# Making a feed-forward pair's weight sums ahead of another operand's chain, and putting off one K tile of wO

## The chip, the cores and the metric

The kernel runs on one core of a Trainium2 chip. The metric is the device time of one execution in microseconds (us), the median of the runs shown. A core has TensorE (PE in the profile, with its weight loads as PEld), VectorE (DVE), ScalarE (ACT), GpSimd (POOL) and SyncE (SP), which issues most DMAs. Each engine takes its instructions in one fixed order and waits on semaphores for the others.

## The reference

One transformer block on 512 tokens of width 1024, in fp32:

```python
h = rmsnorm(x, norm_mix_pre)
... = split_cols(h @ w_in)                       # attention, gated MLP, conv and pool branches, gates
merged = gates[0]*y_a + gates[1]*y_b + gates[2]*y_c + gates[3]*y_d
x = x + rmsnorm(merged @ w_out, norm_mix_post)
h = rmsnorm(x, norm_ffn_pre)
f = jnp.square(jax.nn.relu(h @ w_ff1)) @ w_ff2   # 1024 -> 4096 -> 1024
x = x + rmsnorm(f, norm_ffn_post)
```

The change lies in `merged @ w_out` (in the kernel: wO) and in the first part of the feed-forward layer.

## The kernel before, in words

Every fp32 operand is split in two parts, a rounded high part (`wh`, `hh`, `uh`, ..., made by an ACT cast) and the rest (`wl`, `hl`, `ul`, ..., made by a DVE subtraction). A product is three matmuls, high by high, high by low and low by high (`mm3`). `split_w` makes such a pair of a weight tile of 128x1024 that `load` has brought into one of three `raw` buffers; `wh` and `wl` have five buffers each. Every one of these casts has the line L95 in the profile, that of a helper, so rows are told apart by the names of their tiles.

wO: for each half of the output columns (`hf`) four weight tiles are loaded and split, and for each of four token tiles t, 24 matmuls (8 K tiles by three) run into a PSUM bank `wo`. The left operand of K tile k is the merged activation `mT[k]` (`mh`, `ml`); the one of k = 7 is the last that the gates' loop makes, by a chain of DVE operations on `g` (L538, L540), an ACT cast to `mh` and a DVE subtraction to `ml` (L544).

Then the feed-forward layer. The first four blocks of 128 features (`EARLY = 4`) are made in the plain way: `ff1` runs on the first 256 tokens while the norm of the last token tile is under way, and on the other 256 tokens after it (PSUM tiles `z`). The other 28 blocks are made in pairs by `seven`, a scheme of seven products in place of eight for two feature blocks by two halves of K by two halves of the tokens. It needs sums of the activations (`hsum`, made by `halve`, and `S4`) and sums of the weights. The weights of a pair are loaded as `left` and `rght`; each is split as it is (`w`, `w22`), then four DVE subtractions in place (L344 to L347) turn both into sums, and these are split again (`wl`, `wr`; as tiles also called `wh` and `wl`). PE then runs the parts `pa` (A11 by w), `pb` (A12 by w), `pc` (S1 by the sums of left), `pa` (S2 by the sums of rght), `pd` (A22), `pc` (S4 by `w22`), `pa` (S3). S4 is made before the loop, in two halves in the buffers of `u[-2:]` (called `u30` and `u31` in the order below), by three DVE steps each (L962 to L964), and cast and split into a free part of `h2` (`hh`, `hl`, L973). Between the parts of a pair, `second()` runs the second feed-forward matmul of an earlier block (PSUM tiles `acc`); in the first pair after the parts n = 1, 2 and 4.

Only PE's order (and ACT's in one early stage) is that of the program. On DVE and ACT a scheduler sets it before the run, by the order in the program and its own estimate of when each operand is ready. So what stands earlier in the program tends to be earlier on the engine, and an operation in an engine's order holds back all that stand behind it.

Of the kernel before, what the change touches and what calls it, by code (L numbers as in the profile page):

```python
# [13 lines left out]
AF = mybir.ActivationFunctionType  # L14
# [4 lines left out]
P = 128  # L19
S = 512  # L20
NT = S // P
D = 1024
KD = D // P
# [57 lines left out]
def build(ctx, tc, d, out):  # L81
# [20 lines left out]
    PE, ACT = InOrder(nc.tensor, True), InOrder(nc.scalar, False)  # L102

    def f(t):
        return t.bitcast(F32)
# [4 lines left out]
    def load(src, n=1024):  # L110
        raw = wp.tile([P, 1024], F32, tag="raw", name="raw", bufs=3)
        nc.sync.dma_start(raw[:, :n], src)
        return raw

    def split_w(raw, n=1024):
        hi = wp.tile([P, 1024], F32R, tag="wh", name="wh", bufs=5)
        lo = wp.tile([P, 1024], F32R, tag="wl", name="wl", bufs=5)
        ACT.copy(hi[:, :n], raw[:, :n])
        DVE.tensor_tensor(lo[:, :n], raw[:, :n], f(hi)[:, :n], ALU.subtract)  # L119
        return hi, lo  # L120
# [14 lines left out]
    def weights(src, n=1024):  # L135
        return split_w(load(src, n), n)

    def mm3(ps, lhs, rhs, start, stop, more=False):

        k = dict(skip_group_check=more)  # L140
        PE.matmul(ps, lhs[0], rhs[0], start=start, stop=False, **k)
        PE.matmul(ps, lhs[0], rhs[1], start=False, stop=False, **k)
        PE.matmul(ps, lhs[1], rhs[0], start=False, stop=stop, **k)

    def sl(pair, *ix):
        return pair[0][ix], pair[1][ix]
# [26 lines left out]
    def k0(n):  # L173
        return c0[:, C0[n][0]:C0[n][1]]
# [11 lines left out]
    def bank(name):  # L186
        return mm.tile([P, 512], F32, tag="mm", name=name)

    ps = bank("warm")
# [94 lines left out]
    for (a, b), xt, wa in zip(groups, xts, was):  # L284
        if a == 1:
            angles = rope_tables()
        for k in range(a, b):
            g = k0("gpre")[:, k:k + 1]
# [39 lines left out]
    HK, HS = KD // 2, S // 2  # L328
    B1, B2 = slice(0, 512), slice(512, 1024)

    def part(ps, w, at, a, first):

        for k in range(HK):
            mm3(ps[:, :HS], sl(w, slice(None), slice(at + k * P, at + (k + 1) * P)), sl(a, slice(None), k),
                first and k == 0, k == HK - 1, not first)

    def seven(srcs, forms, small, g, h, by_dma):

        A11, A12, A22, S1, S2, S3, S4 = forms
        left, rght = load(srcs[0]), load(srcs[1])  # L340
        w = split_w(left)
        w22 = split_by_dma(srcs[1][:, B2], rght[:, B2], 512) if by_dma else split_w(rght[:, B2], 512)

        DVE.tensor_tensor(left[:, B1], rght[:, B1], left[:, B1], ALU.subtract)  # L344
        DVE.tensor_tensor(rght[:, B1], rght[:, B2], rght[:, B1], ALU.subtract)
        DVE.tensor_tensor(rght[:, B2], rght[:, B2], left[:, B1], ALU.subtract)
        DVE.tensor_tensor(left[:, B2], left[:, B2], rght[:, B2], ALU.subtract)  # L347
        wl = split_w(left)
        wr = split_w(rght)
        pa, pb = bank("pa"), bank("pb")  # L350
        part(pa, w, 0, A11, True)
        x1 = small()
        ACT.copy(x1, pa[:, :HS])
        yield
        part(pb, w, 512, A12, True)
        DVE.tensor_tensor(g[:, :HS], pb[:, :HS], x1, ALU.add)
        yield
        pc = bank("pc")
        part(pc, wl, 0, S1, True)
        x5 = small()  # L360
        ACT.copy(x5, pc[:, :HS])
        yield
        part(pa, wr, 512, S2, False)
        x2 = small()
        ACT.copy(x2, pa[:, :HS])
        yield
        pd = bank("pd")
        part(pd, wl, 512, A22, True)
        yield
        part(pc, w22, 0, S4, False)  # L370
        DVE.tensor_tensor(h[:, :HS], pc[:, :HS], x2, ALU.add)
        yield
        part(pa, wr, 0, S3, False)
        x3 = small()
        ACT.copy(x3, pa[:, :HS])
        DVE.tensor_tensor(g[:, HS:], pd[:, :HS], x3, ALU.add)  # L376
        DVE.tensor_tensor(h[:, HS:], x3, x5, ALU.add)
        yield
# [245 lines left out]
    ps = bank("kr")  # L624
# [7 lines left out]
    for t in range(NT):  # L632
        ps = bank("q")
# [6 lines left out]
    for j in range(2):  # L640
        ps = bank("kn")
# [3 lines left out]
    for t in range(NT):  # L645
        ps = bank("v")
# [3 lines left out]
    for j in range(3):  # L650
        ps = bank("qT")
# [88 lines left out]
    mT = [], []  # L740
# [19 lines left out]
    def rest(steps):  # L760
        for _ in steps:
            pass
# [39 lines left out]
    ops = forms(z, zsum)  # L802
    w = split_by_dma(d["wB"][1], own=wbp)
    for b in range(2, KD):
        steps = merge(b - 1, w)
        for i in (0, 2):
            g, h = (gp.tile([P, S], F32, tag="g", name="g", bufs=6) for _ in range(2))
            for n, _ in enumerate(seven((d["wG"][4 * b + i], d["wG"][4 * b + i + 1]), ops, small_g, g, h, True)):
                if i == 0 and n in (1, 2, 4, 5):
                    next(steps)  # L810
                if i == 0 and n == 5:
                    rest(steps)
                    w = split_by_dma(d["wB"][b], own=wbp)
            for x in (g, h):
                DVE.tensor_tensor(x, x, rbc, ALU.mult)  # L815
            gates.extend((g, h))
# [36 lines left out]
    def ff1(j, w, ps, lo, hi):  # L853

        for c, parts in ((0, (0, 1)), (1, (0,))):
            for k in range(KD):
                for p in parts:
                    PE.matmul(ps[:, lo:hi], w[c][:, k * P:(k + 1) * P], h2[p][:, k, lo:hi],
                              start=c == 0 and k == 0 and p == 0, stop=c == 1 and k == KD - 1)

    def turn_h(t):
# [14 lines left out]
        DVE.tensor_scalar(stt[:, t, 3:4], stt[:, t, 3:4], 1.0 / D, EPS, ALU.mult, ALU.add)  # L876
        DVE.reciprocal(r2[:, t:t + 1], stt[:, t, 3:4])

    for hf in range(2):
        wo = [weights(d["wO"][hf, c]) for c in range(4)]  # L880
        for t in range(NT):
            ps = bank("wo")
            for k in range(KD):
                mm3(ps, sl([m[k] for m in mT], slice(None), slice(t * P, (t + 1) * P)),
                    sl(wo[k // 2], slice(None), slice((k % 2) * 512, (k % 2 + 1) * 512)), k == 0, k == KD - 1)
            cols = slice(hf * 512, (hf + 1) * 512)
            sq = wk_.tile([P, D], F32, tag="sq", name="sq", bufs=1)
            ACT.activation(sq[:, :512], ps, AF.Square, accum_out=stt[:, t, hf:hf + 1])
            DVE.tensor_tensor(yg[:, t, cols], ps, gmix[:, cols], ALU.mult)
            if hf == 0:  # L890
                DVE.tensor_scalar(stt[:, t, 0:1], stt[:, t, 0:1], D * EPS, None, ALU.add)
                continue
            if t:
                turn_h(t - 1)
            norm_scale(stt[:, t, 2:3], stt[:, t, 3:4], stt[:, t, 0:1], stt[:, t, 1:2])
            for c in (slice(0, 512), slice(512, D)):
                DVE.scalar_tensor_tensor(x1[:, t, c], yg[:, t, c], stt[:, t, 2:3], x1[:, t, c], ALU.mult, ALU.add)
                DVE.tensor_tensor(yg[:, t, c], x1[:, t, c], gffn[:, c], ALU.mult)
    EARLY = 4
    early = []  # L900
    for j in range(EARLY):
        if j == EARLY - 1:
            turn_h(NT - 1)
        w, ps = (split_by_dma if j < 2 else weights)(d["w1"][j]), bank("z")
# [20 lines left out]
    u = [up.tile([P, S], F32, name=f"u{j}") for j in reversed(range(NFF))][::-1]  # L925
# [4 lines left out]
    pend = []  # L930

    def usplit(j):
        uh = us.tile([P, S], F32R, tag="uh", name="uh")
        ul = us.tile([P, S], F32R, tag="ul", name="ul")
        ACT.copy(uh, u[j])
        DVE.tensor_tensor(ul, u[j], f(uh), ALU.subtract)  # L936
        return uh, ul
# [15 lines left out]
    def finish(j):  # L953
        ACT.activation(u[j], u[j], AF.Relu)
        ACT.activation(u[j], u[j], AF.Square)
        pend.append((j, usplit(j)))


    s4 = [x.rearrange("p (k t) -> p k t", k=2) for x in u[-2:]]
    for k, x in zip((0, 2), s4):  # L960
        a, b = slice(HK + k, HK + k + 2), slice(k, k + 2)
        DVE.tensor_tensor(x, f(hh_)[:, a, :HS], f(hsum[0])[:, 1, b], ALU.subtract)  # L962
        DVE.tensor_tensor(x, x, f(hl_)[:, a, :HS], ALU.add)
        DVE.tensor_tensor(x, x, f(hsum[1])[:, 1, b], ALU.subtract)  # L964
    for j, w, ps in early:
        ff1(j, w, ps, HS, S)
        ACT.activation(u[j], ps, AF.Relu)
        ACT.activation(u[j], u[j], AF.Square)
        pend.append((j, usplit(j)))
    for k, x in zip((0, 2), s4):  # L970
        q = sl(h2, slice(None), slice(k, k + 2), slice(HS, S))
        ACT.copy(q[0], x)
# [4 lines left out]
    def small():  # L977
        return fx.tile([P, HS], F32, tag="x", name="x", bufs=5)

    ops = forms(h2, hsum)  # L980
    for j in range(EARLY, NFF, 2):
        g, h = u[j], u[j + 1]
        for n, _ in enumerate(seven((d["w1"][j], d["w1"][j + 1]), ops, small, g, h, False)):
            if n == 4 or n in (1, 2) and j == EARLY:
                second()
        while pend:
            second()
        if j == NFF - 2:
            ahead_u = usplit(0)
        finish(j)  # L990
        finish(j + 1)

    acc2 = [bank("acc2") for _ in range(NT)]
    w = weights(d["w2"][1, 0])
# [19 lines left out]
    for j in range(1, NFF):  # L1014
        if j % 2 == 0:
            w = weights(d["w2"][1, j // 2])
# [100 lines left out]
```

## Time and profile before

| | |
|---|---|
| median of 3 runs | 734.48 us (734.0 to 734.92) |
| the profiled execution's own time | 736.25 us |
| its span, first to last instruction | 734.5 us |
| PE busy | 719.9 us, 98% |
| DVE busy | 532.5 us, 72% |
| ACT busy | 404.8 us, 55% |
| mean granted TensorE clock | 0.993 of full speed |

The span lies 1.75 us below the profiled execution's own time; the rest is outside the first and last instruction. PE is busy nearly all the time, so only time in which it waits, or runs at a lower granted clock, can be had without taking work away. Where that is, the waits and the timeline of PE tell.

### The profile page before, as it was taken

To read this page: it belongs to the slowest core of one execution; us is meant where nothing else is said; L and a number is where in the kernel's file an instruction comes from. 1 tells how busy PE (TensorE), PEld (TensorE's weight loads), DVE (VectorE), ACT (ScalarE), POOL (GpSimd) and SP (SyncE) were. 2 spreads that over 40 slices of the span, in tenths; PEclk is the share of its full clock that TensorE was granted. 3 is DMA by queue.
4 is the path that set the end of the run, shared out by engine and by line. 5 is a ranking of instruction groups with operands and counts; after the bars stand their busy time and mean duration, and the time that the engine had idled before them with its cause. 6 is when DMAs were issued, how large, how long until landed. Compare 5 with 4: busy or idle time off the path is not lost.

```text
span 734.5 us, 11480 instructions
## 1 busy us (share of the span) xinstructions
PE 719.9 (98%) x4490; PEld 648.3 (88%) x4490; DVE 532.5 (72%) x887; ACT 404.8 (55%) x681; POOL 30.4 (4%) x49
## 2 busy tenths in 40 slices
PE   8999999999999999999999899999999999999996
PEld 7998888888999999997889799999999999888885
DVE  6599986985788888986378857766777767764514
ACT  6876443654556665662456545465654656753411
POOL 1110000000101100000010000000000000000001
PEclk9999999999999999999999899999999999999999
DMA  8533222242546645658323123323332243533103
GB/s 304 183 115 116 87 87 60 85 116 72 132 112 158 144 143 131 172 151 308 118 59 112 58 86 102 100 87 122 108 104 99 87 119 111 182 106 114 58 1 114
DMA packets 26182, 86.71 MB, mean 118 GB/s; under 512 B 3344, under 2 KB 3856, under 8 KB 26128
## 3 DMA queue, kind: packets, MB, share of 16 engines
q1 hardware_dynamic: 23072, 78.12, 31.9%
q0 software_dynamic: 3056, 7.87, 6.4%
q8 instruction: 35, 0.57, 0.3%
q14 instruction: 19, 0.16, 0.1%
HBM read 83.87 MB, written 2.10 MB: 117 GB/s over the span
## 4 chain that ended last, share of the span: by engine, by line
PE 71%; DVE 19%; ACT 4%; DMA 3%; issue 2%; SPq 0%; POOL 0%; DVEq 0%; ACTq 0%
PE acc L95 24%; PE pa L95 10%; PE fb L95 9%; PE pc L95 7%; PE wo L95 5%; DVE wl L119 5%; PE pd L95 3%; PE pb L95 3%; PE y L95 2%; ACT wh L95 2%; PE psA L95 2%; PE sgv L95 2%; PE z L95 1%; DMA raw<-in_wG 1%; DVE g L540 1%
## 5 line engine op out<-in xcount | busy, mean ns | idle before, releaser
L95 ACT CAST wh<-raw 128x1024 fp32r<-128x1024 f32 (+2 forms) x171 | 165.3, 980 | 145.8 <-PE pc L95 52.6
L119 DVE TENSOR_TENSOR wl<-raw,wh 128x1024 fp32r<-128x1024 f32 (+2 forms) x157 | 181.7, 1169 | 41.8 <-ACT wh L95 39.2
L95 PE MATMUL acc<-wh,uh 128*128 128x512 f32 x232 | 91.4, 394 | 0.0
L95 PE MATMUL acc<-wl,uh 128*128 128x512 f32 x232 | 91.3, 394 | 0.0
L95 PE MATMUL acc<-wh,ul 128*128 128x512 f32 x232 | 91.1, 393 | 0.0
L936 DVE TENSOR_TENSOR ul<-u,uh 128x512 fp32r<-128x512 f32 x58 | 38.6, 689 | 58.2 <-ACT uh L95 58.2
L95 PE MATMUL fb<-zh,wh 128*128 128x512 f32 x144 | 56.7, 394 | 0.1
L95 PE MATMUL fb<-zh,wl 128*128 128x512 f32 x144 | 56.2, 390 | 0.1
L95 PE MATMUL fb<-zl,wh 128*128 128x512 f32 x144 | 56.1, 390 | 0.0
L95 ACT CAST uh<-u 128x512 fp32r<-128x512 f32 x58 | 34.3, 617 | 35.3 <-PE acc L95 33.7
L95 PEld LDWEIGHTS acc<-wh,ul 128*128 128x128 f32 x232 | 44.0, 190 | 9.8 <-DVE ul L936 0.4
L95 PEld LDWEIGHTS acc<-wh,uh 128*128 128x128 f32 x232 | 44.1, 190 | 8.8 <-ACT uh L95 0.4
L95 PEld LDWEIGHTS acc<-wl,uh 128*128 128x128 f32 x232 | 44.0, 190 | 8.1
L95 ACT ACTIVATE u<-u 128x512 f32<-128x512 f32 x60 | 33.1, 621 | 17.7 <-DVE u L376 17.7
L95 ACT COPY x<-pa 128x256 f32<-128x256 f32 x78 | 28.4, 366 | 8.8 <-PE pa L95 7.2
L95 PEld LDWEIGHTS fb<-zh,wl 128*128 128x128 f32 x144 | 27.0, 188 | 6.2 <-DVE wl L119 0.5
L95 PEld LDWEIGHTS fb<-zh,wh 128*128 128x128 f32 x144 | 27.1, 188 | 5.7 <-DVE zc L429 0.4
L95 PEld LDWEIGHTS fb<-zl,wh 128*128 128x128 f32 x144 | 27.1, 188 | 5.3
L95 PE MATMUL pa<-hsh,wh 128*128 128x256 f32 x112 | 31.2, 279 | 0.0
L95 PE MATMUL pa<-hsl,wh 128*128 128x256 f32 x112 | 31.2, 279 | 0.0
L95 PE MATMUL pa<-hsh,wl 128*128 128x256 f32 x112 | 31.2, 279 | 0.0
L95 ACT ACTIVATE g<-g,c 128x512 f32<-128x512 f32 x32 | 22.5, 721 | 10.4 <-DVE g L815 10.3
(391 smaller groups left out, 1997.0 us busy)
## 6 DMA issues: line engine op xcount, KB each, us to landing
raw<-in_w SPq DMA_DIRECT2D x64, 512.0 KB, 3.5
raw<-in_wG SPq DMA_DIRECT2D x32, 512.0 KB, 3.5
raw<-in_wF SPq DMA_DIRECT2D x10, 512.0 KB, 3.9
raw<-in_wB SPq DMA_DIRECT2D x8, 512.0 KB, 4.7
raw<-in_wO SPq DMA_DIRECT2D x8, 512.0 KB, 4.2
bl<-in_wB POOLq DMA_DIRECT2D x7, 512.0 KB, 7.7
wl<-in_wG POOLq DMA_DIRECT2D x12, 256.0 KB, 4.3
xk<-in_x SPq DMA_DIRECT2D x4, 512.0 KB, 9.5
```

The source lines that it names most:

```text
L95: ins = op(*a, **k)
L119: DVE.tensor_tensor(lo[:, :n], raw[:, :n], f(hi)[:, :n], ALU.subtract)
L540: DVE.tensor_tensor(g, g, prev, ALU.add)
L936: DVE.tensor_tensor(ul, u[j], f(uh), ALU.subtract)
```

## The change

Two edits. In wO's first half the first two token tiles are taken together: the K tiles 0 to 6 of both, then K tile 7 of both (`wo_tiles`, `both`). And `seven` is cut in two: `seven_w`, a generator, makes the weights of a pair, their splits and sums, in three steps, and `seven` takes what it made. For the first pair its first step stands ahead of the second token half of the early blocks, and its other two behind the `ff1` of the blocks j = 2 and 3; the loop over the early blocks, which stood between the two stages of S4, now stands ahead of both.

```diff
-    def seven(srcs, forms, small, g, h, by_dma):
-
-        A11, A12, A22, S1, S2, S3, S4 = forms
+    def seven_w(srcs, by_dma):
+
         left, rght = load(srcs[0]), load(srcs[1])
         w = split_w(left)
         w22 = split_by_dma(srcs[1][:, B2], rght[:, B2], 512) if by_dma else split_w(rght[:, B2], 512)
...
         DVE.tensor_tensor(left[:, B2], left[:, B2], rght[:, B2], ALU.subtract)
-        wl = split_w(left)
-        wr = split_w(rght)
+        yield w, w22
+        yield split_w(left)
+        yield split_w(rght)
+
+    def seven(ws_, forms, small, g, h):
+
+        A11, A12, A22, S1, S2, S3, S4 = forms
+        (w, w22), wl, wr = ws_
         pa, pb = bank("pa"), bank("pb")
...
+    def wo_tiles(ps, wo, t, a, b):
+        for k in range(a, b):
+            mm3(ps, sl([m[k] for m in mT], slice(None), slice(t * P, (t + 1) * P)),
+                sl(wo[k // 2], slice(None), slice((k % 2) * 512, (k % 2 + 1) * 512)), k == 0, k == KD - 1)
+
     for hf in range(2):
         wo = [weights(d["wO"][hf, c]) for c in range(4)]
+
+        both = 2 if hf == 0 else 0
+        wops = [bank("wo") for _ in range(both)]
+        for ka, kb in ((0, KD - 1), (KD - 1, KD)):
+            for t in range(both):
+                wo_tiles(wops[t], wo, t, ka, kb)
         for t in range(NT):
-            ps = bank("wo")
-            for k in range(KD):
-                mm3(ps, sl([m[k] for m in mT], slice(None), slice(t * P, (t + 1) * P)),
-                    sl(wo[k // 2], slice(None), slice((k % 2) * 512, (k % 2 + 1) * 512)), k == 0, k == KD - 1)
+            if t < both:
+                ps = wops[t]
+            else:
+                ps = bank("wo")
+                wo_tiles(ps, wo, t, 0, KD)
...
+    first = seven_w((d["w1"][EARLY], d["w1"][EARLY + 1]), False)
+    first_w = [next(first)]
+    for j, w, ps in early:
+        ff1(j, w, ps, HS, S)
+        ACT.activation(u[j], ps, AF.Relu)
+        ACT.activation(u[j], u[j], AF.Square)
+        pend.append((j, usplit(j)))
+        if j >= EARLY - 2:
+            first_w.append(next(first))
 
     s4 = [x.rearrange("p (k t) -> p k t", k=2) for x in u[-2:]]
     for k, x in zip((0, 2), s4):
...
         DVE.tensor_tensor(x, x, f(hsum[1])[:, 1, b], ALU.subtract)
-    for j, w, ps in early:
-        ff1(j, w, ps, HS, S)
-        ACT.activation(u[j], ps, AF.Relu)
-        ACT.activation(u[j], u[j], AF.Square)
-        pend.append((j, usplit(j)))
     for k, x in zip((0, 2), s4):
...
-        for n, _ in enumerate(seven((d["w1"][j], d["w1"][j + 1]), ops, small, g, h, False)):
+        for n, _ in enumerate(seven(first_w if j == EARLY else list(seven_w((d["w1"][j], d["w1"][j + 1]), False)),
+                                      ops, small, g, h)):
```

The gates' loop calls the two functions in the same way, with `list(seven_w(...))`. The orders of SP and POOL stay as they were.

PE's order in wO's first half, from K tile 6 of the first token tile on; `wo_3834` is the bank of the first token tile and `wo_3863` that of the second, `mh7` and `ml7` the two parts of K tile 7. Before:

```order
L95 MATMUL wo_3834<-wl_3831,mh6_1887 128x512
L95 MATMUL wo_3834<-wh_3830,ml6_1888 128x512
L95 MATMUL wo_3834<-wh_3830,mh7_1889 128x512
L95 MATMUL wo_3834<-wl_3831,mh7_1889 128x512
L95 MATMUL wo_3834<-wh_3830,ml7_1890 128x512
L95 MATMUL wo_3863<-wh_3812,mh0_1645 128x512
L95 MATMUL wo_3863<-wl_3813,mh0_1645 128x512
L95 MATMUL wo_3863<-wh_3812,ml0_1646 128x512
```

After, at the end of the two tiles taken together, where `wo_3835` is the second token tile's bank and `wo_3892` the third's:

```order
L95 MATMUL wo_3835<-wl_3831,mh6_1887 128x512
L95 MATMUL wo_3835<-wh_3830,ml6_1888 128x512
L95 MATMUL wo_3834<-wh_3830,mh7_1889 128x512
L95 MATMUL wo_3834<-wl_3831,mh7_1889 128x512
L95 MATMUL wo_3834<-wh_3830,ml7_1890 128x512
L95 MATMUL wo_3835<-wh_3830,mh7_1889 128x512
L95 MATMUL wo_3835<-wl_3831,mh7_1889 128x512
L95 MATMUL wo_3835<-wh_3830,ml7_1890 128x512
L95 MATMUL wo_3892<-wh_3812,mh0_1645 128x512
L95 MATMUL wo_3892<-wl_3813,mh0_1645 128x512
```

The 21 matmuls of the second token tile on K tiles 0 to 6 now stand between K tile 6 of the first one and the first use of K tile 7.

DVE's order from the last step of S4's sums to the first pair's `wl` of left; `raw_4507` is left and `raw_4509` rght, `u30` and `u31` the halves of S4. Before:

```order
L936 TENSOR_TENSOR ul_4407<-u0_4359,uh_4406 128x512
L936 TENSOR_TENSOR ul_4437<-u1_4358,uh_4436 128x512
L973 TENSOR_TENSOR hl_3790<-u30_4329,hh_3789 128x2x256
L936 TENSOR_TENSOR ul_4467<-u2_4357,uh_4466 128x512
L344 TENSOR_TENSOR raw_4507<-raw_4509,raw_4507 128x512
L973 TENSOR_TENSOR hl_3790<-u31_4328,hh_3789 128x2x256
L345 TENSOR_TENSOR raw_4509<-raw_4509 128x512
L356 TENSOR_TENSOR u4_4355<-pb_4532,x_4545 128x256
L346 TENSOR_TENSOR raw_4509<-raw_4509,raw_4507 128x512
L347 TENSOR_TENSOR raw_4507<-raw_4507,raw_4509 128x512
L936 TENSOR_TENSOR ul_4497<-u3_4356,uh_4496 128x512
L119 TENSOR_TENSOR wl_4524<-raw_4507,wh_4523 128x1024
```

After, from right behind the subtraction of `w22` on, where left is `raw_4374`, rght `raw_4376` and the lines are those of the changed file:

```order
L343 TENSOR_TENSOR raw_4374<-raw_4376,raw_4374 128x512
L989 TENSOR_TENSOR u30_4329<-hh_3789,hsh_3791 128x512
L344 TENSOR_TENSOR raw_4376<-raw_4376 128x512
L990 TENSOR_TENSOR u30_4329<-u30_4329,hl_3790 128x512
L345 TENSOR_TENSOR raw_4376<-raw_4376,raw_4374 128x512
L954 TENSOR_TENSOR ul_4417<-u0_4359,uh_4416 128x512
L346 TENSOR_TENSOR raw_4374<-raw_4374,raw_4376 128x512
L954 TENSOR_TENSOR ul_4447<-u1_4358,uh_4446 128x512
L954 TENSOR_TENSOR ul_4477<-u2_4357,uh_4476 128x512
L991 TENSOR_TENSOR u30_4329<-u30_4329,hsl_3792 128x512
L119 TENSOR_TENSOR wl_4481<-raw_4374,wh_4480 128x1024
L989 TENSOR_TENSOR u31_4328<-hh_3789,hsh_3791 128x512
```

The four sums (`raw`) now alternate with S4's first half and the early blocks' splits, and S4's second half stands behind the `wl` of left.

ACT's order from the third early block's first activation on, before; `wh_4523` and `wh_4527` are the casts of the sums, `wh_4628` that of the next tile of w2:

```order
L95 ACTIVATE u2_4357<-z_4236 128x512
L95 CAST hh_3789<-u30_4329 128x2x256
L95 ACTIVATE u2_4357<-u2_4357 128x512
L95 ACTIVATE u3_4356<-z_4287 128x512
L95 CAST uh_4466<-u2_4357 128x512
L95 ACTIVATE u3_4356<-u3_4356 128x512
L95 CAST hh_3789<-u31_4328 128x2x256
L95 COPY x_4545<-pa_4531 128x256
L95 CAST uh_4496<-u3_4356 128x512
L95 CAST wh_4523<-raw_4507 128x1024
L95 CAST wh_4527<-raw_4509 128x1024
L95 CAST wh_4628<-raw_4626 128x1024
```

After, where the casts of the sums are `wh_4480` and `wh_4514`:

```order
L95 ACTIVATE u2_4357<-z_4236 128x512
L95 ACTIVATE u2_4357<-u2_4357 128x512
L95 ACTIVATE u3_4356<-z_4287 128x512
L95 CAST uh_4476<-u2_4357 128x512
L95 CAST wh_4480<-raw_4374 128x1024
L95 ACTIVATE u3_4356<-u3_4356 128x512
L95 CAST wh_4514<-raw_4376 128x1024
L95 CAST hh_3789<-u30_4329 128x2x256
L95 COPY x_4545<-pa_4531 128x256
L95 CAST wh_4628<-raw_4626 128x1024
L95 CAST uh_4510<-u3_4356 128x512
L95 COPY x_4585<-pc_4572 128x256
```

Both casts of the sums moved ahead of S4's casts, and the cast of the first `u3` split moved behind that of w2's next tile.

## Rows read from the trace of the kernel before

**Rows 1.** The page's busy times: us, share of the span, instructions.
```profile
PE 719.9 (98%) x4490; PEld 648.3 (88%) x4490; DVE 532.5 (72%) x887; ACT 404.8 (55%) x681; POOL 30.4 (4%) x49
```
**Rows 2.** Waits of PE from 325 to 440 us: total, times, longest.
```profile
PE pc L95 <- ACT wh L95: 2.5, 1, 2.5
PE wo L95 <- ACT mh L95: 1.0, 1, 1.0
PE pc L95 <- DVE wl L119: 0.8, 1, 0.8
```
**Rows 3.** Timeline of PE in wO: start, duration, operation [idle before].
```profile
341.84 0.39 PE L95 MATMUL wo<-wh,ml 128*128 128x512 f32 x1
343.27 0.50 PE L95 MATMUL wo<-wh,mh 128*128 128x512 f32 x1 [1.04 <-ACT mh L95]
...
344.57 0.39 PE L95 MATMUL wo<-wl,mh 128*128 128x512 f32 x1
```
**Rows 4.** Timeline of DVE, the end of the chain of K tile 7.
```profile
343.25 0.69 DVE L544 TENSOR_TENSOR ml<-g,mh 128x512 fp32r<-128x512 f32 x1 [0.68 <-ACT mh L95]
```
**Rows 5.** Timeline of PE around the first pair of `seven`.
```profile
408.49 0.28 PE L95 MATMUL pa<-hh,wh 128*128 128x256 f32 x1
...
413.81 0.39 PE L95 MATMUL acc<-wh,ul 128*128 128x512 f32 x1
416.67 0.38 PE L95 MATMUL pc<-hsh,wh 128*128 128x256 f32 x1 [2.48 <-ACT wh L95]
...
417.93 0.58 PE L95 MATMUL pc<-hsh,wl 128*128 128x256 f32 x1 [0.76 <-DVE wl L119]
...
424.82 0.28 PE L95 MATMUL pa<-hsh,wh 128*128 128x256 f32 x1
...
430.36 0.28 PE L95 MATMUL pc<-hh,wh 128*128 128x256 f32 x1
```
**Rows 6.** Chain of waits, undisturbed parts of the next pair: start, length, matmuls.
```profile
433.32 2.75 PE acc L95 x12
...
438.87 1.40 PE pc L95 x12
```
**Rows 7.** Windows: length, busy time of PE, PEld, DVE, ACT, POOL; granted clock, DMA.
```profile
345.00:384.00 39.00, 39.00 (x181) 32.44 (x180) 19.86 (x37) 16.82 (x31) 3.33 (x5) 1.00 0.34 105
...
404.00:409.00 5.00, 5.00 (x45) 5.00 (x45) 5.00 (x9) 3.20 (x7) 0.00 (x0) 1.00 0.00 0
418.00:420.20 2.20, 2.20 (x10) 2.20 (x11) 2.15 (x2) 0.52 (x1) 0.00 (x0) 0.50 0.41 119
420.20:424.00 3.80, 3.80 (x11) 3.01 (x10) 0.00 (x0) 0.37 (x1) 0.00 (x0) 0.50 0.86 332
440.00:620.00 180.00, 180.00 (x1268) 168.19 (x1267) 129.55 (x179) 104.78 (x175) 0.00 (x0) 1.00 0.32 102
```
**Rows 8.** Timeline of DVE ahead of the first pair's sums.
```profile
405.97 1.28 DVE L962 TENSOR_TENSOR u<-hh,hsh 128x512 f32<-128x512 f32 x2
...
414.13 0.68 DVE L346 TENSOR_TENSOR raw<-raw 128x512 f32<-128x512 f32 x1
414.85 0.69 DVE L347 TENSOR_TENSOR raw<-raw 128x512 f32<-128x512 f32 x1
...
416.65 3.50 DVE L119 TENSOR_TENSOR wl<-raw,wh 128x1024 fp32r<-128x1024 f32 x3 [0.51 <-ACT wh L95]
```
**Rows 9.** Timeline of ACT in the same stretch.
```profile
409.15 0.62 ACT L95 CAST hh<-u 128x512 fp32r<-128x512 f32 x1 [1.96 <-DVE u L964]
...
415.57 2.94 ACT L95 CAST wh<-raw 128x1024 fp32r<-128x1024 f32 x3 [0.91 <-DVE raw L347]
```
**Rows 10.** Timeline of POOL: issue of the DMA that completes a `wl`.
```profile
383.19 0.89 POOL L132 DMA_DIRECT2D wl<-in_w  x1 [1.68 <-ACT wl L95]
```
**Rows 11.** DMA issues from 383 to 385 us: count, KB each, us to landing.
```profile
wl<-in_w POOLq DMA_DIRECT2D x1, 512.0 KB, 6.4
```
**Rows 12.** Timeline of PE: the first use of that `wl`.
```profile
389.84 0.52 PE L95 MATMUL z<-hh,wl 128*128 128x256 f32 x3
```

More of the change, by code (lines that the diff above doesn't have):

```diff
@@ L807, in build @@
             g, h = (gp.tile([P, S], F32, tag="g", name="g", bufs=6) for _ in range(2))
-            for n, _ in enumerate(seven((d["wG"][4 * b + i], d["wG"][4 * b + i + 1]), ops, small_g, g, h, True)):
+            for n, _ in enumerate(seven(list(seven_w((d["wG"][4 * b + i], d["wG"][4 * b + i + 1]), True)),
+                                              ops, small_g, g, h)):
                 if i == 0 and n in (1, 2, 4, 5):
```

## The prediction

> **What bounds the kernel now.** I read the page's busy times first: PE is busy for 719.9 of 734.5 us [rows 1], so this kernel gets faster only where PE stands still or runs slowly. Then PE's waits in the stretch that the diff touches: three, of 2.5, 1.0 and 0.8 us, two at the first pair's `pc` and one at wO [rows 2]. PE's timeline gives what they really cost, since an idle time is not yet the delay.
>
> At wO the last matmul ahead of K tile 7 starts at 341.84. Undisturbed, 12 matmuls of 512 columns take 2.75 us [rows 6], 0.229 each, so the next was due at 342.07. The fifth, that one counted, starts at 344.57 [rows 3] and was due at 342.07 + 4 x 0.229 = 342.99. PE leaves this place 1.58 us late.
>
> At the first pair the last `acc` matmul ahead of `pc` starts at 413.81, so `pc` was due at 414.04. Its 12 matmuls take 1.40 us and the 12 of `acc` behind them 2.75 when undisturbed [rows 6], so `pa` was due at 418.19; it starts at 424.82 [rows 5]. PE leaves this place 6.63 us late. Two things make this up. The third matmul of `pc`, the first that needs `wl`, starts at 417.93 and was due two matmuls of 0.117 behind 414.04, at 414.27: 3.66 us of waiting. And the granted clock, 1.00 before, is 0.50 (1.2 in place of 2.4 GHz) from 418.0 to 424.0 behind the wait [rows 7]: 6.0 us at half speed are 3.0 us lost, and 6.63 - 3.66 = 2.97 agrees. In the rest PE has no gap: 39.00 of 39.00 us from 345 to 384, 180.00 of 180.00 from 440 to 620, at clock 1.00 [rows 7]. So 1.58 + 6.63 = 8.21 us is the most that the change can have.
>
> Why `pc` waits: DVE is busy without a gap from 404 to 409 [rows 7] and beyond, and does S4's six steps and the early splits ahead of the four weight sums. The last sum starts at 414.85 [rows 8], ACT casts the sums from 415.57, having waited for it [rows 9], and DVE subtracts from 416.65.
>
> **wO, part by part.** No matmul is added; 21 of them, 21 x 0.229 = 4.81 us, come between K tile 6 of the first token tile and the first use of K tile 7, which moves from 342.07 to 346.88. `mh` is there by 343.27 [rows 3], since PE starts then, and `ml` by 343.25 + 0.69 = 343.94 [rows 4]. Both are early by some 3 us, so the 1.58 us go. The first token tile is complete 4.8 - 1.6 + 0.7 = some 4 us after its due time; its readers are ACT and DVE operations off PE's path, and no bank for a third or fourth tile was waited for before [rows 2]. What the trace doesn't show as such is PE going to and fro between two open banks. The nearest row is `acc`, which changes bank after every three matmuls and still takes 2.75 us for 12 [rows 6], against 0.23 a matmul in wO: between 0 and 0.02 us a change, with three changes. I take 0. Bounds of this edit: 0 (all of it lost again behind) to 1.58; I take 1.58.
>
> **The sums, part by part.** The work on DVE and ACT stays the same; only its order changes. DVE starts S4's first step at 405.97 before [rows 8]; in that place now stands the first sum. Left and rght have long been cast and split there (the subtraction of `w22` stands right ahead). By the order, ten half-width subtractions now precede `wl` of left: four sums, three S4 steps, three early splits. Two in a row take 1.28 us and one 0.68 [rows 8], so starts are 0.60 apart. The last sum is the seventh: 405.97 + 6 x 0.60 + 0.68 = 410.25. ACT must be free then: it stood idle for 1.96 us until 409.15, waiting for S4 [rows 9], whose cast is no longer ahead of it; what remains is three pieces of about 0.6, one of which needs the last early matmuls, over about when `pa` starts, at 408.49 [rows 5]; so it is free by 409.9, and casts left by 410.3 + 1.0 = 411.3 (three casts take 2.94 [rows 9]). DVE gets to `wl` at 405.97 + 10 x 0.60 = 411.97 and ends by 413.2 (three take 3.50 [rows 8], and one alone 1.2). PE needs it at 414.27. Cover: 1.1 us, and the 3.66 us wait goes. Without a wait ahead of it, nothing in the trace lets the clock fall there, so the 2.97 go with it.
>
> What is late next, in PE's order: `wl` of rght, one half-width step behind, ends at 413.1 + 0.6 + 1.2 = 414.9, for `pa` at 418.19. The next tile of w2 follows four half-width steps and one of half that width later, 414.9 + 2.4 + 0.4 + 1.2 = 418.9, for the `acc` behind `pd` at 418.19 + 1.40 + 1.40 = 420.99. S4's second half, now behind that, ends at 419.5, for the second `pc` at 420.99 + 2.75 = 423.74 (it was at 430.36 [rows 5], hence early enough before as now). Smallest cover behind the first: 2.1 us. On ACT the cast of w2's next tile now stands ahead of the last early `uh`; that `uh` needs a buffer which the first `acc` frees only at its end, near 414.0, so it gets hardly later. The loads into left's and rght's buffers are issued as DVE lets them go, some 3.5 us sooner, on an SP queue whose order is unchanged. Bounds of this edit: 0 (the wait only changes its name) to 6.63; between them 3.66 with the slow clock staying. I take 6.63, the nearest to rows that all show cover.
>
> A rule speaks against it. The row above shows starts 0.60 apart where one lasts 0.68: neighbours overlap. The Trainium skill (VectorE: DVE Perf Modes, The DRAIN you can't avoid) says that the next operation starts only when the one before has left the pipeline. By the rule the ten steps would take 10 x 0.68 = 6.8 in place of 6.0, `wl` would end at 414.0, and the cover would shrink from 1.1 to 0.3 us; the sum would stay. The trace has it otherwise, but this is why a rival below keeps a chance.
>
> **Sum.** 736.25 (the profiled execution: span 734.5 and 1.75 around it) - 1.58 - 6.63 = 728.04. That execution lies 1.77 above the median of the runs shown, 734.48; against the median the same 8.21 give 726.3.
>
> **Rivals.**
> 1. The clock's part isn't had (7 in 100). The runs without a profile are 1.3 to 2.3 us faster, so perhaps the clock doesn't fall in them, or it falls in the changed kernel too. Against it: the three runs lie within 0.92 us of each other. 734.48 - 8.21 + 2.97 = 729.2.
> 2. The sums are late again (7 in 100). DVE has no gap left, and a cover of 1.1 us is less than one full-width subtraction; if one more stood ahead, or starts were 0.68 apart and a cast late by half a microsecond, PE would wait 0.2 to 1.5 us again, up to 3 more if the clock falls: 726.5 to 730.8. Against it: the order lists each of the ten steps.
> 3. wO's part is given back (6 in 100). A `wl` that a DMA of POOL completes is issued at 383.19 [rows 10], lands 6.4 later [rows 11], at 389.59, and PE uses it at 389.84 [rows 12]: 0.25 us of cover. If that issue didn't move up with PE, PE would wait 1.58 - 0.25 = 1.33 there: 727.6. Against it: the issue follows an ACT operation, which stands behind ACT's reading of a wO bank.
> 4. Slower, by S4 (2 in 100). Its second half is cut off from its first, and stands on DVE and ACT behind operations that wait for PE. If its end came at T, the second `pc` would wait T - 423.74, and 3.0 more with the clock. That outweighs the 8.21 from T = 428.95 on, 9.5 us later than reckoned; at T = 432, 726.3 + 8.3 + 3.0 = 737.6. Against it: nothing ahead of it waits for PE later than 416.
> 5. The change doesn't do what it says for the sums (2 in 100): some operand not seen here keeps them where they were, and only wO gains: 734.48 - 1.58 = 732.9.
>
> **How the numbers follow.** The forecast, 726.3, has the remaining 76 in 100, with its own range of 725.5 to 727.3 from the spread of the runs shown and the bounds of the small terms. The range 724.9 to 729.5 takes in rivals 1 and 3 and half of 2. A measurement of this kernel can tell about 0.2%, 1.5 us, from no change, so faster means below 733.0: forecast, rivals 1 to 3 and nearly all of 5, 95 in 100. Same: 3, slower: 2.
>
> **What would show it.** In the changed profile: no PE wait at wO or `pc`, granted clock 1.00 through the first pair; the first pair's `wl` of left done about 1 us ahead of `pc`, and from the start of that `pc` to that of the `pa` behind it 1.40 + 2.75 = 4.15 us, where it was 424.82 - 416.67 = 8.15 [rows 5]. The prediction is wrong if `pc` still names DVE or ACT as releaser, if the clock still falls to 0.50, or if PE waits anew between 345 and 400 or at the second `pc`.

## The result, and the profile after

The changed kernel takes 727.17 us, median of 4 runs (726.9 to 727.96), beside 734.7 for the kernel before on the same chip. The ratio is 0.9898, 95% interval 0.9881 to 0.9915: 7.5 us (6.2 to 8.7) faster. The forecast was 726.3, the range 724.9 to 729.5. Two later batches gave medians of 727.19 and 727.13, and the forecast lies below all 15 runs of the three batches (lowest 726.53). The predicted gain of 8.21 us still lies within the interval, so this comparison alone doesn't show that a term was off; the experiments below do. The mechanism came as predicted, and the term of the sum for the slow clock was too large, by some 1 to 2 us.

The profiled execution took 727.39 us (span 725.7), 8.86 less than that of before. I read the page's busy times first, as in [rows 1].

```profile
PE 715.5 (99%) x4490; PEld 646.0 (89%) x4490; DVE 532.4 (73%) x887; ACT 405.6 (56%) x681; POOL 31.4 (4%) x49
```

Every engine has as many instructions as before; PE's share rose to 99%. PE's waits over the whole span are these (total, times, longest):

```profile
PE warm L95 <- DVE warm L164: 1.1, 1, 1.1
PE psA L95 <- ACT wah L95: 1.1, 1, 1.1
PE psA L95 <- DVE wah L290: 0.9, 1, 0.9
PE pT L95 <- ACT p L95: 0.4, 1, 0.4
```

The three of [rows 2] are gone, and none of these lies near the edits. At wO, PE's timeline (start, duration, operation, idle time before it in brackets) now runs through, where [rows 3] showed 1.04 us of waiting. These are the first uses of the first token tile's `mh` and `ml` of K tile 7:

```profile
346.24 0.39 PE L95 MATMUL wo<-wh,mh 128*128 128x512 f32 x1
...
346.69 0.39 PE L95 MATMUL wo<-wh,ml 128*128 128x512 f32 x1
```

The chain of K tile 7 is no earlier relative to PE; it is only needed later. The timelines of ACT and DVE give its end:

```profile
342.06 0.62 ACT L95 CAST mh<-g 128x512 fp32r<-128x512 f32 x1 [3.58 <-DVE g L545]
...
342.71 0.69 DVE L549 TENSOR_TENSOR ml<-g,mh 128x512 fp32r<-128x512 f32 x1 [0.69 <-ACT mh L95]
```

`mh` is there at 342.68 and `ml` at 343.40. wO begins at 336.72 in this trace and 42 matmuls stand ahead of K tile 7, so `mh` is first used 9.52 us later, at 346.24, and `ml` two matmuls behind it, at 346.69: 3.3 us of cover (predicted some 3). Without the edit `mh` would have been due 21 matmuls earlier, at 341.48, and would not have been there.

At the first pair, PE's timeline answers to [rows 5]:

```profile
406.30 0.28 PE L95 MATMUL pa<-hh,wh 128*128 128x256 f32 x1
...
411.84 0.28 PE L95 MATMUL pc<-hsh,wh 128*128 128x256 f32 x1
...
412.08 0.28 PE L95 MATMUL pc<-hsh,wl 128*128 128x256 f32 x1
...
415.99 0.28 PE L95 MATMUL pa<-hsh,wh 128*128 128x256 f32 x1
...
421.53 0.28 PE L95 MATMUL pc<-hh,wh 128*128 128x256 f32 x1
```

From `pc` to the `pa` behind it are 4.15 us, the predicted number (8.15 before). From the first `pa` to the second are 9.69 us, where it was 424.82 - 408.49 = 16.33: 6.64 us less, against a predicted 6.63. The windows (length, busy time of PE, PEld, DVE, ACT, POOL, then granted clock and DMA) show 1.00 where [rows 7] had 0.50:

```profile
418.00:420.20 2.20, 2.20 (x16) 1.94 (x15) 2.13 (x4) 0.62 (x1) 0.00 (x0) 1.00 0.61 214
420.20:424.00 3.80, 3.80 (x29) 3.57 (x28) 2.15 (x4) 0.98 (x1) 0.00 (x0) 1.00 0.00 0
440.00:610.00 170.00, 170.00 (x1198) 158.84 (x1197) 121.52 (x167) 100.28 (x167) 0.00 (x0) 1.00 0.33 103
```

DVE's timeline, beside [rows 8], shows the sums between S4's steps and early splits:

```profile
403.78 0.69 DVE L343 TENSOR_TENSOR raw<-raw 128x512 f32<-128x512 f32 x1
404.38 0.69 DVE L989 TENSOR_TENSOR u<-hh,hsh 128x512 f32<-128x512 f32 x1
404.98 0.69 DVE L344 TENSOR_TENSOR raw<-raw 128x512 f32<-128x512 f32 x1
...
407.39 0.68 DVE L346 TENSOR_TENSOR raw<-raw 128x512 f32<-128x512 f32 x1
...
409.80 1.22 DVE L119 TENSOR_TENSOR wl<-raw,wh 128x1024 fp32r<-128x1024 f32 x1
...
411.54 1.22 DVE L119 TENSOR_TENSOR wl<-raw,wh 128x1024 fp32r<-128x1024 f32 x1
...
415.41 1.22 DVE L119 TENSOR_TENSOR wl<-raw,wh 128x1024 fp32r<-128x1024 f32 x1
...
416.55 0.68 DVE L995 TENSOR_TENSOR hl<-u,hh 128x512 fp32r<-128x512 f32 x1
```

`wl` of left ends at 411.02 and is first used at 412.08: 1.06 us of cover, predicted 1.1. The other three ends are 412.76 for the `pa` of 415.99 (3.2; predicted 3.3), 416.63 for the `acc` that PE's timeline has at 418.79 (2.2; predicted 2.1), and 417.23 for the `pc` of 421.53 (4.3; predicted 4.2). ACT, beside [rows 9], casts left right behind the last sum, which ends at 408.07:

```profile
408.11 1.06 ACT L95 CAST wh<-raw 128x1024 fp32r<-128x1024 f32 x1 [0.50 <-DVE raw L346]
```

POOL's issue of [rows 10] moved up with PE. POOL's timeline, and PE's at the first use:

```profile
381.00 0.88 POOL L132 DMA_DIRECT2D wl<-in_w  x1 [1.69 <-ACT wl L95]
...
387.65 1.10 PE L95 MATMUL z<-hh,wl 128*128 128x256 f32 x8
```

With the 6.3 us to landing that the list of DMA issues gives it, `wl` is there at 387.3, and PE first uses it at 387.65. The issue moved up by 2.19 us and so did the use, so the cover is as thin as before: 0.35 us, where it was 0.25.

The two places give 1.58 + 6.64 = 8.22 of the 8.86 us between the two profiled executions. Nearly all of the rest is an earlier start: wO's first matmul stands at 336.72 here and at 337.31 before, 0.59 earlier, ahead of both edits. This is not the change's: two profiled executions of one and the same kernel, the sums alone (below), have it at 337.50 and 336.41.

### The profile page after: what moved, and what is told of

It reads as the page before. It is cut to its first block, busy times and chain, and to the rows that moved or that the text cites. A ratio compares the mean times of both kernels' runs of the same rounds, so it can differ in the third digit from the quotient of the medians.

```text
span 725.7 us, 11480 instructions
## 1 busy us (share of the span) xinstructions
PE 715.5 (99%) x4490; PEld 646.0 (89%) x4490; DVE 532.4 (73%) x887; ACT 405.6 (56%) x681; POOL 31.4 (4%) x49
## 4 chain that ended last, share of the span: by engine, by line
PE 95%; DVE 3%; DMA 1%; issue 0%; SPq 0%; ACT 0%; DVEq 0%; ACTq 0%
PE acc L95 24%; PE pa L95 15%; PE fb L95 12%; PE pc L95 10%; PE y L95 6%; PE wo L95 6%; PE pb L95 5%; PE pd L95 5%; PE z L95 3%; PE psA L95 2%; PE sgv L95 2%; PE po L95 1%; DMA wA<-in_wA 1%; PE tr L95 1%; PE s L95 1%; PE q L95 1%
```

## The experiments

My theory after the result: the gain is two delays of PE that go, wO's (1.58) and the pair's wait (3.66), and the slow clock behind that wait, which costs 2.97 in the profiled execution of before but less in a typical run. The rival: the clock costs nothing in runs without a profile, and the gain above 5.2 comes from elsewhere. A second rival: the parts don't add up, because one gives the other's time back. Gains below are (1 - ratio) times the median of the kernel before in the same batch, with the 95% interval.

**wO alone.** The kernel before with wO's edit:

```
+        both = 2 if hf == 0 else 0
+        wops = [bank("wo") for _ in range(both)]
+        for ka, kb in ((0, KD - 1), (KD - 1, KD)):
+            for t in range(both):
+                wo_tiles(wops[t], wo, t, ka, kb)
```

> Only the wO edit; the first pair's weight sums stay where they were before. Theory (two separate delays of PE add up, 1.58 us at wO and 6.63 at the first pair): 1.58 us faster than before, about 733.0 us, with PE's wait at wO gone and the one at the first pair unchanged (3.6 us, then granted clock 0.50). Rival (wO's part is given back further on, which would also explain that the two edits together brought 7.5 us and not 8.2): within 0.5 us of before, 734.1 to 734.7, and a new or longer wait of PE between wO and the first pair.

> The wO edit alone, timed again beside the other two kernels of this batch. If the parts add up (the two alone give together what both give), then it gains 7.4 less what the sums alone gain here. If wO's part is partly lost again while the pair still waits, the two alone give together over 1 us less than both: about 1.1 for this one, 4.9 for the sums, 7.4 for both.

Measured: 732.93 us (11 runs), ratio 0.9985 [0.9976, 0.9994], a gain of 1.1 (0.4 to 1.8); again, 733.33 (12 runs), 0.9979 [0.9965, 0.9993], 1.5 (0.5 to 2.6). wO's wait is gone and the pair's two stay. No new wait appears between wO and the pair, so nothing gave wO's part back there. The two profiled executions of this one program turned out to be the most telling of all. PE's timeline at the pair in the first:

```profile
406.37 0.28 PE L95 MATMUL pa<-hh,wh 128*128 128x256 f32 x1
...
414.56 0.39 PE L95 MATMUL pc<-hsh,wh 128*128 128x256 f32 x1 [2.49 <-ACT wh L95]
...
415.82 0.58 PE L95 MATMUL pc<-hsh,wl 128*128 128x256 f32 x1 [0.76 <-DVE wl L119]
...
422.61 0.28 PE L95 MATMUL pa<-hsh,wh 128*128 128x256 f32 x1
```

And in the second:

```profile
406.09 0.28 PE L95 MATMUL pa<-hh,wh 128*128 128x256 f32 x1
...
414.26 0.39 PE L95 MATMUL pc<-hsh,wh 128*128 128x256 f32 x1 [2.48 <-ACT wh L95]
...
415.53 0.58 PE L95 MATMUL pc<-hsh,wl 128*128 128x256 f32 x1 [0.76 <-DVE wl L119]
...
421.03 0.28 PE L95 MATMUL pa<-hsh,wh 128*128 128x256 f32 x1
```

The waits are the same to 0.01 us, and the first matmul that needs `wl` starts 9.45 and 9.44 us behind the first `pa`. What follows differs: from it to the second `pa` 6.79 us in the one and 5.50 in the other, where the changed kernel takes 415.99 - 412.08 = 3.91. The windows say why; the first execution from 416 us on:

```profile
416.00:418.00 2.00, 2.00 (x10) 2.00 (x11) 2.00 (x2) 0.40 (x1) 0.00 (x0) 0.50 0.58 150
418.00:420.00 2.00, 2.00 (x7) 1.61 (x7) 0.03 (x1) 0.37 (x1) 0.00 (x0) 0.50 0.93 268
420.00:422.00 2.00, 2.00 (x7) 1.56 (x6) 0.00 (x0) 0.00 (x0) 0.00 (x0) 0.54 0.88 336
```

And the second:

```profile
416.00:418.00 2.00, 2.00 (x11) 2.00 (x11) 1.74 (x2) 0.11 (x1) 0.00 (x0) 0.50 0.61 217
418.00:420.00 2.00, 2.00 (x9) 1.58 (x8) 0.00 (x0) 0.37 (x1) 0.00 (x0) 0.82 0.81 254
420.00:422.00 2.00, 2.00 (x15) 1.78 (x14) 0.00 (x0) 0.77 (x1) 0.00 (x0) 1.00 0.82 313
```

Behind the same wait the clock comes back from 1.2 to 2.4 GHz over 2 us sooner, and the loss is 1.59 us in place of 2.88. So the clock's part isn't the same in every execution.

**The sums alone.** The changed kernel without wO's edit:

```
-        both = 2 if hf == 0 else 0
+        both = 0
```

> Only the sums made ahead; wO as before. Theory: 6.63 us faster than before, about 728.0 us, wait at wO still there (1.0 us), none at the first pair, granted clock 1.00 there. Rival (the clock falls only in profiled executions, so the wait of 3.66 us is all there is): 3.7 us faster, about 730.9 us.

> The sums alone, on the same chip. Parts that add up: 5.8 of gain or so beside 1.6 for wO. Parts that don't: 4.9, and 1.1 for wO.

Measured: 729.25 us (6 runs), 0.9933 [0.9918, 0.9948], a gain of 4.9 (3.8 to 6.0); again, 729.18 (5 runs), 0.9927 [0.9911, 0.9943], 5.4 (4.2 to 6.5). Both intervals lie below the 6.63 of the theory and above the 3.66 of the wait alone. So timed runs do lose something to the clock, but less than the 2.97 of the profiled execution: 1.3 and 1.7 by these medians. Of the three waits before, PE has only wO's left. Its timeline there in the first, to be read as [rows 3]:

```profile
342.03 0.39 PE L95 MATMUL wo<-wh,ml 128*128 128x512 f32 x1
344.09 0.50 PE L95 MATMUL wo<-wh,mh 128*128 128x512 f32 x1 [1.67 <-ACT mh L95]
...
345.40 0.40 PE L95 MATMUL wo<-wl,mh 128*128 128x512 f32 x1
```

By the prediction's reckoning the fifth matmul was due at 342.03 + 5 x 0.227 = 343.17 and starts at 345.40: wO costs 2.23 us in this execution, not 1.58. In the second one it is 1.83 by the same reckoning (343.90 against 342.07).

**The changed kernel beside them.**

> The changed kernel once more, beside more runs of the one before. Alone, the wO edit brought 1.1 us and the sums 4.9, 6.0 together, where both in one kernel had brought 7.5 against few runs. Theory now (the two parts add up; the clock's part of the second is smaller in timed runs than the 2.97 us of the profiled one, because the clock falls for a shorter time in most of them): 6.0 to 7.0 us faster than before, 727.3 to 728.3 us. Rival (the parts help each other, or all 8.2 us are there): 7.5 to 8.2 us faster.

> The changed kernel on the same chip: 7.4 of gain by either theory; it is the sum against which the two parts are held.

Measured: 727.19 us (6 runs), 0.9901 [0.9881, 0.9921], a gain of 7.3 (5.8 to 8.7), which lies between the two expectations and decides nothing; and 727.13 (5 runs), 0.9903 [0.9885, 0.9920], 7.1 (5.9 to 8.5). In the batch that held all three, wO alone and the sums alone give 1.5 + 5.4 = 6.9 beside 7.1 for both: the parts add up, and the second rival is out as far as these intervals tell.

**The wait kept, the clock held.** The kernel before, with 28 matmuls of 256 columns put on PE where it would stand still. They write the bank that `pc` then overwrites, so nothing else changes:

```
     def seven(srcs, forms, small, g, h, by_dma, fill=0):
...
+        for _ in range(fill):
+            PE.matmul(pc[:, :HS], w[0][:, :P], A11[0][:, 0], start=True, stop=True)
         part(pc, wl, 0, S1, True)
```

> The kernel before, with 28 matmuls of 256 columns (3.3 us at full clock) put on PE ahead of the first pair's first pc, into the bank that pc overwrites: PE has work while it waits for the sums, which come no earlier. Theory (the wait itself costs 3.66 us, and the fall of the clock behind it another 2.97): granted clock stays 1.00, about 3.0 us faster than before, 731.6 us. Rival (the clock's part is not in the timed runs, or the clock falls for another reason): 734.6 us, or a clock of 0.50 in the same place.

Measured: 732.95 us (12 runs), 0.9985 [0.9971, 0.9999], a gain of 1.1 (0.1 to 2.1). PE's timeline:

```profile
414.61 3.43 PE L95 MATMUL pc<-hh,wh 128*128 128x256 f32 x28
...
418.53 0.38 PE L95 MATMUL pc<-hsh,wl 128*128 128x256 f32 x1 [0.26 <-DVE wl L119]
...
422.55 0.28 PE L95 MATMUL pa<-hsh,wh 128*128 128x256 f32 x1
```

The first `pa` starts at 409.07 in this execution, so `wl` is used 9.46 us behind it, as late as before (9.44), and the second `pa` follows 4.02 us later in place of 6.89. The window of this stretch shows the clock held:

```profile
412.00:430.00 18.00, 17.75 (x118) 16.07 (x117) 13.09 (x19) 7.61 (x12) 0.00 (x0) 1.00 0.26 88
```

Matmuls that compute nothing make the kernel faster, though the interval reaches down to 0.1. With the sums alone, this puts the first rival out: the clock costs something in runs without a profile too. The gain lies between the two expectations, and its interval ends below the 2.87 us between the two profiled executions.

**The same filler with wO's edit.** The kernel before with wO's edit and the filler, that is, the changed kernel but for the sums, which stay late under a held clock:

```
+        for _ in range(fill):
+            PE.matmul(pc[:, :HS], w[0][:, :P], A11[0][:, 0], start=True, stop=True)
```

> The wO edit, and the 28 matmuls on PE ahead of the first pair's first pc, with the sums where they were before: the clock is held, and the wait of 3.66 us stays. Theory: gains of the wO edit and of the held clock add up, 1.1 to 1.6 and 1.1 to 3.0 us: 2.2 to 4.6 us faster than before, and 3.66 slower than the changed kernel, some 731 us. Granted clock 1.00 at the first pair. Rival (the clock's part is not there in timed runs): 1.1 to 1.6 us faster than before, 732.7 us, and 5 us or more slower than the changed kernel.

Measured: 731.32 us (10 runs), 0.9956 [0.9941, 0.9971], a gain of 3.2 (2.1 to 4.3) as expected, and 4.1 us above the changed kernel's 727.19 in its batch. In its profile the first `pa` to the second takes 13.50 us, against 9.69: 3.81 more. This is the wait by itself, 3.66 in the prediction. The gain is 1.7 to 2.1 above the 1.5 and 1.1 of wO alone: a second price for the clock, from other batches than wO's.

**Sums made later.** The changed kernel with 2, 3 or 4 further half-width operations on left behind the fourth sum. With 2 or 4 they add and subtract the same; with 3 the fourth sum is off by one addition, so the kernel no longer computes the reference's function.

```
+        for c in range(late):
+            DVE.tensor_tensor(left[:, B2], left[:, B2], rght[:, B2], ALU.subtract if c % 2 else ALU.add)
```

> The changed kernel with two more half-width operations on the first pair's left sums (add and subtract the same again), which by the order of VectorE put the low part of left's sums three half-width steps, 1.8 us, later: 412.8 us where PE needs it at 412.1. Theory (cover of 1.06 us; beyond it each us late is a us of the end): PE waits 0.75 us at the first pair, time 0.7 to 0.8 above the changed kernel, about 727.9 us, if the clock holds over so short a wait. If it falls as it did behind the wait of before: 3 us more, about 730.9 us. Rival (the first pair's sums are not what PE waits for by now, the cover is larger than the rows say): 727.2 us, no wait.

> The changed kernel with three more half-width operations on the first pair's left sums (the sum comes out one rght off, so this product is not the reference's), which by VectorE's order put the low part of left's sums five half-width steps, 3.0 us, later: PE waits 3.0 - 1.06 = 1.95 us at the first pair. Theory (each us beyond the cover is a us): 1.95 us above the changed kernel if the clock holds, up to 3 us more if it falls as it did behind the 3.66 us of before; the profile tells which. Rival: no more than two more operations cost (0.6 to 1.0 us).

> The changed kernel with four more half-width operations on the first pair's left sums (the same added and subtracted twice), which by VectorE's order put the low part of left's sums eight half-width steps, 4.8 us, later: PE waits 4.8 - 1.06 = 3.75 us at the first pair, as long as before the change. Theory: the whole delay of before is back by this alone, 3.75 us and the fall of the clock behind it: granted clock 0.50 for some us behind the wait, time 5 to 6.7 us above the changed kernel, about that of the kernel with the wO edit alone, 733 us. Rival (the clock fell for another reason than the wait): 3.75 us above the changed kernel, 731 us, clock 1.00.

Measured: 728.15 us with 2 (4 runs, 0.9918 [0.9906, 0.9931]), 730.09 with 3 (7 runs, 0.9938 [0.9912, 0.9964]), 732.93 with 4 (12 runs, 0.9979 [0.9967, 0.9991]). PE's timeline with 2:

```profile
412.53 0.38 PE L95 MATMUL pc<-hsh,wl 128*128 128x256 f32 x1 [0.64 <-DVE wl L119]
...
416.55 0.28 PE L95 MATMUL pa<-hsh,wh 128*128 128x256 f32 x1
```

With 3:

```profile
413.24 0.39 PE L95 MATMUL pc<-hsh,wh 128*128 128x256 f32 x1 [0.82 <-ACT wh L95]
...
414.50 0.38 PE L95 MATMUL pc<-hsh,wl 128*128 128x256 f32 x1 [0.76 <-DVE wl L119]
...
420.12 0.28 PE L95 MATMUL pa<-hsh,wh 128*128 128x256 f32 x1
```

With 4:

```profile
414.27 0.39 PE L95 MATMUL pc<-hsh,wh 128*128 128x256 f32 x1 [2.03 <-ACT wh L95]
...
416.13 0.58 PE L95 MATMUL pc<-hsh,wl 128*128 128x256 f32 x1 [1.36 <-DVE wl L119]
...
421.68 0.28 PE L95 MATMUL pa<-hsh,wh 128*128 128x256 f32 x1
```

In the batch of the last two the changed kernel took 727.19, so 3 cost 2.9 us and 4 cost 5.7. With 4 the gain over the kernel before is 1.5 us, that of wO's edit alone (1.1 and 1.5): what the sums' edit gained is gone again by their lateness alone.

The windows show the clock, with 2 and then with 3:

```profile
412.00:430.00 18.00, 17.47 (x115) 15.99 (x116) 14.14 (x20) 9.75 (x17) 0.00 (x0) 1.00 0.42 128
...
416.00:418.00 2.00, 2.00 (x7) 1.52 (x6) 2.00 (x5) 0.62 (x2) 0.00 (x0) 0.50 0.85 285
```

The profiled executions with a wait at the pair can now be laid side by side; the other four without one, of the changed kernel and of the sums alone, agree with the first row to 0.01 us. "Late" is the time from the first `pa` to the first use of `wl`, less the changed kernel's 412.08 - 406.30 = 5.78. "Clock" is the time from there to the second `pa`, less its 3.91.

| kernel | PE's waits at `pc`, us | late, us | clock, us |
|---|---|---|---|
| changed | none | 0 | 0 |
| 2 more operations | 0.64 | 0.81 | 0.11 |
| 3 more | 0.82 + 0.76 | 2.01 | 1.71 |
| 4 more | 2.03 + 1.36 | 3.82 | 1.64 |
| before | 2.48 + 0.76 | 3.66 | 2.98 |
| wO alone, first | 2.49 + 0.76 | 3.67 | 2.88 |
| wO alone, second | 2.48 + 0.76 | 3.66 | 1.59 |
| before with filler | 0.26 | 3.68 | 0.11 |
| wO and filler | 0.25 | 3.68 | 0.13 |

With 2 operations PE is 0.81 us late. DVE's rows there have `wl` 4.21 us behind the last sum (411.25 and 407.04), 1.80 more than the changed kernel's 2.41: three steps of 0.60, the two added ones and one of S4's, which now slips in ahead of `wl`. Less the cover of 1.06 that is 0.74, near the 0.81: the cover is real, and used up as reckoned. Behind waits of 0.26 and 0.64 us the clock stays at 1.00, so the 0.11 to 0.13 in the last column there are not the clock's. Behind 0.82 + 0.76 us and more it falls, and the loss doesn't grow with the wait (1.64 behind 3.4 us, 2.98 behind 3.2). The five losses lie in two groups, 1.59 to 1.71 and 2.88 to 2.98, with none between.

**The clock over the timed runs.** The three batches ran the kernel before 62 times, and each run has a mean granted clock of its own. For scale, the profiled execution of before, at 736.25 us, had 0.993.

| mean granted clock | runs | mean time, us |
|---|---|---|
| 0.991 | 2 | 739.0 |
| 0.993 and 0.994 | 19 | 735.4 |
| 0.995 | 21 | 734.5 |
| 0.997 | 13 | 733.9 |
| 0.999 | 7 | 732.5 |

From 0.999 to 0.993 are 2.9 us, as much as the clock's part in the profiled execution. The median of all 62 is 734.44, which is 1.9 above the runs at 0.999. The changed kernel's runs in the two later batches are all between 0.997 and 0.999. This grouping shows how the two move together and not which causes which, and among the changed kernel's runs, with no wait at the pair, those at 0.999 (726.9 to 728.0) are no faster than those at 0.997 (726.5 to 727.5). So the 1.9 is an estimate; the two executions of wO alone, above, show at the pair what lies behind it.

## Why the prediction was right, and where it was off

**What bounds the kernel.** Right. The waits named were the only ones that mattered; PE is busy for 99% of the span without them.

**wO.** The mechanism was right: the wait goes, and the going to and fro between two open banks costs nothing, since wO's matmuls start 0.227 apart across the whole stretch. The size was read from one execution. The same delay is 1.58, 2.23 and 1.83 us in the profiled executions of before and of the sums alone, and 2.00 in that of the filler, a mean of 1.91. Timed, the edit alone gave 1.1 and 1.5, and on top of the sums 729.18 - 727.13 = 2.1. By the profiled executions the term was some 0.3 us too small; the timed runs lie on both sides of it and don't tell.

**The sums: the wait.** Right: 3.66 predicted, 3.81 with the clock held and 4.1 timed. The cover behind it came out as worked out, 1.06 against 1.1, and the three later ones within 0.1.

**The sums: the clock.** Right in kind, wrong in size, and this is the step that failed: "against the median the same 8.21 give 726.3". The 2.97 us in that sum came from an execution at a mean clock of 0.993, which itself lay 1.77 above the median; the prediction noted that distance and went past it. Timed, the sums alone gained 4.9 and 5.4 where the term was 6.63, which leaves 1.3 and 1.7 for the clock; the filler gave 1.1 and 1.7 to 2.1, the grouping by clocks 1.9. So a median run of before loses 1 to 2 us to the clock (an estimate), and not 2.97. With the largest of these and wO's mean, 1.91 + 3.66 + 1.9 = 7.5, the measured gain; with the smaller ones and wO's timed 1.1 to 1.5 the sum is 6 to 7. If wO's term was too small, the two errors cancel in part, and the forecast's nearness is in part luck.

**The rule against it.** DVE's rows of the changed kernel start 0.60 apart where each lasts 0.68 or 0.69 (403.78, 404.38, 404.98). By the rule of the Trainium skill (VectorE: DVE Perf Modes, The DRAIN you can't avoid) they would have been 0.68 apart or more. The trace doesn't have it so for these independent neighbours. The same section of the Trainium skill allows for it in the sentence that ends its first paragraph, which the prediction left out: a next operation that is not held starts earlier.

**The rivals.** The first, that the clock's part isn't had (729.2), holds in part: by the figures above a third to two thirds of the 2.97 are not had. The second, sums late again (726.5 to 730.8), is what 2 and 3 more operations do, and their 728.15 and 730.09 lie in its range: the cover was 1.06 us and no more. The third, wO's part given back at POOL's `wl`, didn't come, since the issue and PE's use both moved up by 2.19 us; its cover of 0.35 us stays the thinnest here. The fourth, slower by S4, is out with 4.3 us of cover, and the fifth with the order seen in DVE's rows. The prediction's 95 in 100 for faster isn't the sum of its parts: 76, 7, 7, 6 and nearly all of 2 are some 98.

**What stays open.** Why the clock comes back sooner in one execution than in another behind the same wait; no run here tells, and a timed run's loss to it is known only as 1 to 2 us. Nor why wO's delay varies by 0.6 us; I didn't follow its chain of loads through the runs. None of these kernels beat the changed one.

## What to carry to other kernels

Work out what a wait costs from the time at which PE leaves the place, not from the idle time: here idle times of 3.2 us were a delay of 6.6. But where part of that delay is a slow clock, don't take its price from one profiled execution: against the median, subtract only what a median run loses, and look at more than one execution for that. Operations that others wait for belong ahead of those that have time, on an engine that is never idle, and the cover that this buys should be checked against one more operation of that engine.

## What the runs showed of the hardware

The clock's fall behind the same wait lasts differently long: at 0.50 from 418.0 to 424.0 in the profiled execution of before [rows 7] and from 416 to beyond 420 in one of wO alone, but back at 1.00 by 420 in the other. In the five executions in which it fell it cost 1.6 to 1.7 us or 2.9 to 3.0. A wait of 0.64 us left it at 1.00; waits of 0.82 and 0.76, half a us of work apart, did not. 28 matmuls without a use, in a wait of over 3 us, held it at 1.00 and made the kernel 1.1 us faster (0.1 to 2.1).
